# A row-sum kernel whose last load is split in two by partitions

## The chip, the cores and the metric

The kernel runs on one core of a Trainium2 chip. The metric is device time in microseconds of one execution; the kernel before has three such times. Beside them there is one profiled execution, from which all spans, waits and lengths below are taken.

## The reference

The kernel sums the last axis of a float32 array of 32 x 512 x 1024. Seen flat, these are 16,384 rows of 1024 numbers, 67.1 MB to be read, and 16,384 sums, 66 KB, to be written.

```python
def setup_inputs():
    batch, seq, dim = 32, 512, 1024
    return {"x": np.random.randn(batch, seq, dim).astype(np.float32)}

def reference(x):
    return np.sum(x, axis=-1).astype(np.float32)
```

## The kernel before, in words

Each of the 128 partitions owns 128 rows: 112 of the body (`x_a`, results in `res_a`) and 16 of the end (`x_z`, results in `res_z`). The rows of one partition lie one behind the other in memory.

The body goes through three buffers `xt0` to `xt2`, sixteen rows a partition each, seven blocks in all. Every block comes by two loads, of the even and of the odd partitions (64 each), that share one semaphore of the buffer; the very first row of each partition comes ahead of them by a load of its own (`first`). VectorE sums a block with one reduction (`rows_dve`, line 55). In the seventh block ScalarE takes seven of the sixteen rows, one at a time (`rows_act`, line 66).

The end's sixteen rows come in five loads. Three pieces of 9, 4 and 2 rows go into a body buffer (line 94); the last row of each partition goes into a tile of its own, `tail`, in two loads of all 128 partitions (lines 95 to 97): columns 0 to 543, and columns 544 to 1023, the latter 16 places further on so that there is room for a partial sum between them. VectorE and ScalarE share the first two pieces by rows; of the third each takes one row. For the last row VectorE adds the two halves of a stretch to one another and sums the result (`pairs_dve`, line 73, one addition and one read of the accumulator). This is done twice: first for columns 0 to 543, whose sum is written just ahead of the remaining 480 columns, behind a zero in the gap, and then for those 480 columns with that sum and the zero before them (482 numbers, 241 pairs). The second addition therefore waits for its load (line 126) and for VectorE's own earlier result (line 127).

All loads and both stores are issued by SP in the order of the list `loads` (lines 131 to 134): a load into a buffer that was in use waits for the reduction that frees it. The five end loads follow at once on one another, since they go into one freed buffer and into `tail`, which was free from the start. After them SP waits for the first tail load, for the body's sums on VectorE and on ScalarE, and issues the store of `res_a`; then for all sums, and issues the store of `res_z` (lines 135 to 141). At the very end it clears the semaphores. Three of the loads are moved ahead of the program's opening barrier.

Of the kernel before, what the change touches and what calls it, by code (L numbers as in the profile page):

```python
# [10 lines left out]
G = 16  # L11
BUFS = 3
ACT_ROWS = 7
CUT = 544
CUTS = (0, 9, 13, 15)
EARLY = 3


def row_sums(nc, x: bass.AP, out: bass.AP):
    P = nc.NUM_PARTITIONS  # L20
    x_flat = x.flatten_outer_dims()
    R, D = x_flat.shape
# [4 lines left out]
    def block(r0, n):  # L27
        x_b = x_flat[r0 : r0 + P * n].rearrange("(p c) d -> p (c d)", p=P)
        out_b = out_flat[r0 : r0 + P * n].rearrange("(p c) -> p c", p=P)
        return x_b, out_b  # L30

    x_a, out_a = block(0, BODY)
    x_z, out_z = block(P * BODY, G)

    def sbuf(name, n):
        return nc.alloc_sbuf_tensor(name, [P, n], F32)

    xt = [sbuf(f"xt{i}", G * D) for i in range(BUFS)]
    tail = sbuf("tail", D + 16)
# [2 lines left out]
    res_z = sbuf("res_z", G)  # L42

    names = [f"slot{i}" for i in range(BUFS)] + ["first", "piece0", "piece1", "piece2", "tail0"]
    names += ["tail1", "vec", "act", "early_store", "store"]
    sems = {n: nc.alloc_semaphore(n) for n in names}
    slots = [sems[f"slot{i}"] for i in range(BUFS)]
    vec, act = sems["vec"], sems["act"]
# [22 lines left out]
    def pairs_dve(t, a, b, acc, pairs):  # L71
        h = (a + b) // 2
        nc.vector.tensor_tensor_reduce(  # L73
            out=pairs[:, 0 : h - a], in0=t[:, a:h], in1=t[:, h:b], scale=1.0, scalar=0.0,
            op0=ADD, op1=ADD, accum_out=acc,
        ).then_inc(vec, 1)
        count["vec"] += 1
# [5 lines left out]
    loads = []  # L83
    for b in range(n_bufs):
# [4 lines left out]
        for q, i, s in parts:  # L89
            k = 1 if s is sems["first"] else G  # L90
            loads.append((b, xt[b % BUFS][q, i * D : k * D], x_a[q, (c + i) * D : (c + k) * D], s))
    last = xt[n_bufs % BUFS]
    for k, (i, j) in enumerate(zip(CUTS, CUTS[1:])):
        loads.append((n_bufs, last[:, i * D : j * D], x_z[:, i * D : j * D], sems[f"piece{k}"]))
    for k, (i, j, gap) in enumerate(((0, CUT, 0), (CUT, D, 16))):
        e = (G - 1) * D
        loads.append((0, tail[:, i + gap : j + gap], x_z[:, e + i : e + j], sems[f"tail{k}"]))


    nc.vector.memset(tail[:, CUT + 15 : CUT + 16], 0.0).then_inc(vec, 1)  # L100
    count["vec"] += 1
# [11 lines left out]
    for k in range(2):  # L113
        i, j = CUTS[k], CUTS[k + 1]
        h = (j - i) // 2
# [8 lines left out]
    nc.vector.wait_ge(sems["tail0"], 16)  # L124
    pairs_dve(tail, 0, CUT, tail[:, CUT + 14 : CUT + 15], pairs[0])
    nc.vector.wait_ge(sems["tail1"], 16)
    nc.vector.wait_ge(vec, count["vec"])
    pairs_dve(tail, CUT + 14, D + 16, res_z[:, 15:16], pairs[1])

# [19 lines left out]
def kernel(tc: tile.TileContext, x: bass.AP, out: bass.AP):  # L149
    tc.close()  # L150
    tc.compile()  # L151
    nc = tc.nc
    row_sums(nc, x, out)

    sp = mybir.EngineType.SP
    fn = nc.m.functions[0]
    entry, body = None, None
    for blk in fn.blocks:  # L160
        ops = [i for i in blk.instructions if i.engine == sp]
        if entry is None:
            entry = blk
        elif any(i.opcode == "DMACopy" for i in ops):
            body = blk
            break
    code = list(body.instructions)
    loads = [i for i in code if i.engine == sp and i.opcode == "DMACopy"][:EARLY]
    for load in loads:
        assert not load.sync_info.on_wait  # L170
        code.remove(load)
    body.instructions = code
    code = list(entry.instructions)
    at = next(k for k, i in enumerate(code) if i.engine == sp and i.opcode == "Drain")
    code[at:at] = loads
    entry.instructions = code
# [29 lines left out]
```

## Time and profile before

| | us |
|---|---|
| Three executions, median | 162.22 |
| lowest and highest | 161.07, 162.95 |
| Profiled execution, span from its first to its last instruction | 159.6 |
| VectorE busy in it | 121.4 (76%) |
| ScalarE busy in it | 17.2 (11%) |
| Bytes moved, and mean rate over the span | 67.18 MB, 421 GB/s |
| Share of the 16 DMA engines' span that the load and store queue took | 98.1% |
| Issue of the last load, and time to its landing | 118.37, 39.3 |

The span is counted from the first to the last of the program's own instructions; the executions' times also hold what lies around it, 2.6 us by the median. A load's time to landing runs from its issue on SP to the moment when all sixteen increments of its semaphore are there; for loads that are queued behind others most of it is waiting in the queue. Starts in what follows are microseconds from the start of the span.

### The profile page before, as it was taken

The page shows a single profiled execution, that of the slowest core. Times are in us where ns is not written, and L with a number is a line of the kernel's source. Part 1 is how long each engine was busy: PE and PEld are TensorE (multiplying, and loading weights), DVE is VectorE, ACT ScalarE, POOL GpSimd, SP SyncE. Part 2 cuts the span into 40 slices and gives each one's busy share as a digit, 9 for nine tenths or more (in the row PEclk, how much of TensorE's full clock was granted, in tenths as well). Part 3 has the DMA queues.
Part 4 walks back from the last instruction along what each step waited for, and adds up shares of the span by engine and source line. Part 5 has one row for each costly group of instructions (what it writes and reads, how often), then busy time and mean ns, then how long its engine had stood idle before and what let it go on. Part 6 is the DMA issues. An engine that isn't in the chain of part 4 may idle for free.

```text
span 159.6 us, 114 instructions
## 1 busy us (share of the span) xinstructions
DVE 121.4 (76%) x16; ACT 17.2 (11%) x31; POOL 0.2 (0%) x4
## 2 busy tenths in 40 slices
DVE  0000049998699968999599994999949999499685
ACT  2000000000000000000000000000000000494694
POOL 0000000000000000000000000000000000000000
DMA  9988996996996997998969969969969969699994
GB/s 378 493 370 370 493 526 263 526 509 279 526 509 279 526 460 329 526 411 378 526 263 526 526 263 526 526 263 526 509 279 526 509 279 526 296 443 443 390 401 145
DMA packets 2273, 67.18 MB, mean 421 GB/s; under 512 B 609, under 2 KB 737, under 8 KB 993
## 3 DMA queue, kind: packets, MB, share of 16 engines
q1 hardware_dynamic: 2272, 67.18, 98.1%
q14 instruction: 1, 0.00, 0.0%
HBM read 67.11 MB, written 0.07 MB: 421 GB/s over the span
## 4 chain that ended last, share of the span: by engine, by line
DMA 74%; DVE 22%; SPq 2%; issue 0%
DMA xt<-in_x_dram 49%; DMA tail<-in_x_dram 25%; DVE res_a L55 22%; SPq L134 2%; DVE pairs L73 0%; DVE res_z L73 0%
## 5 line engine op out<-in xcount | busy, mean ns | idle before, releaser
L55 DVE TENSOR_REDUCE res_a<-xt 128x16 f32<-128x16384 f32 (+1 forms) x7 | 113.1, 16154 | 31.6 <-DMA xt<-in_x_dram 31.6
L66 ACT ACTIVATE xt<-xt 128x1024 f32<-128x1024 f32 x15 | 15.6, 1044 | 137.5 <-DMA xt<-in_x_dram 137.5
L55 DVE TENSOR_REDUCE res_z<-xt 128x4 f32<-128x4096 f32 (+1 forms) x2 | 6.7, 3353 | 1.8 <-DMA xt<-in_x_dram 1.8
L66 ACT ACTIVATION_READ_ACCUMULATOR xt<-xt 128x1 f32 x15 | 2.8, 188 | 0.0
L100 DVE MEMSET tail<- 128x1 f32 x1 | 0.1, 59 | 3.0 <-PEq L151 3.0
L66 ACT ACT_TABLE_LOAD x1 | 1.3, 1283 | 2.9 <-PEq L151 2.9
L73 DVE CUSTOM_DVE_ANT_0 pairs<-tail 128x272 f32<-128x272 f32 (+1 forms) x2 | 0.9, 427 | 0.1
L73 DVE CUSTOM_DVE_ANT_0 pairs<-xt 128x512 f32<-128x512 f32 x1 | 0.7, 692 | 0.2 <-DMA xt<-in_x_dram 0.2
L73 DVE DVE_READ_ACCUMULATOR2_ANT res_z<- 128x1 f32 x2 | 0.2, 83 | 0.0
L190 POOL MEMSET const-bfloat16-1.0<- 128x1 bf16 x1 | 0.1, 102 | 0.0
L190 POOL MEMSET const-uint8-127<- 128x1 uint8 x1 | 0.1, 102 | 0.0
L190 POOL MEMSET const-float32-1.0<- 128x1 f32 x1 | 0.1, 99 | 0.0
L190 POOL MEMSET const-float32-0.0<- 128x1 f32 x1 | 0.1, 98 | 0.2 <-issue 0.2
L73 DVE DVE_READ_ACCUMULATOR2_ANT tail<- 128x1 f32 x1 | 0.1, 83 | 0.0
## 6 DMA issues: line engine op xcount, KB each, us to landing
xt<-in_x_dram SPq DMA_DIRECT2D x2, 3840.0 KB, 16.6
xt<-in_x_dram SPq DMA_DIRECT2D x1, 4608.0 KB, 32.5
xt<-in_x_dram SPq DMA_DIRECT2D x1, 2048.0 KB, 37.0
xt<-in_x_dram SPq DMA_DIRECT2D x1, 1024.0 KB, 39.0
xt<-in_x_dram SPq DMA_DIRECT2D x1, 512.0 KB, 3.7
tail<-in_x_dram SPq DMA_DIRECT2D x1, 272.0 KB, 39.2
tail<-in_x_dram SPq DMA_DIRECT2D x1, 240.0 KB, 39.3
xt<-in_x_dram SPq DMA_DIRECT2D x12, 39.0
```

The source lines that it names most:

```text
L55: nc.vector.tensor_reduce(out=res[:, c : c + n], in_=t[:, j * D : (j + n) * D].rearrange("p (j d) -> p j d", d=D), axis=X, op=ADD,).then_i ...
L66: nc.scalar.activation(out=v, in_=v, func=COPY, accum_out=res[:, c + i : c + i + 1]).then_inc(act, 1)
L73: nc.vector.tensor_tensor_reduce(out=pairs[:, 0 : h - a], in0=t[:, a:h], in1=t[:, h:b], scale=1.0, scalar=0.0, op0=ADD, op1=ADD, accum_out ...
L100: nc.vector.memset(tail[:, CUT + 15 : CUT + 16], 0.0).then_inc(vec, 1)
L134: nc.sync.dma_start(out=dst, in_=src).then_inc(s, 16)
L190: nc = _bacc.Bacc("TRN2", target_bir_lowering=False, num_devices=1)
```

## The change

The second load of the last row, columns 544 to 1023 of all 128 partitions, is replaced by two: first partitions 120 to 127, then partitions 0 to 119. The second of them has a new semaphore, `tail2`, and VectorE's last addition waits for it too. Nothing else is touched: the tiles, the bytes, the other loads and the store's conditions stay.

```diff
+WIDE = 120
...
-    names += ["tail1", "vec", "act", "early_store", "store"]
+    names += ["tail1", "tail2", "vec", "act", "early_store", "store"]
...
-    for k, (i, j, gap) in enumerate(((0, CUT, 0), (CUT, D, 16))):
-        e = (G - 1) * D
-        loads.append((0, tail[:, i + gap : j + gap], x_z[:, e + i : e + j], sems[f"tail{k}"]))
+    e = (G - 1) * D
+    ends = ((0, CUT, 0, slice(0, P)), (CUT, D, 16, slice(WIDE, P)), (CUT, D, 16, slice(0, WIDE)))
+    for k, (i, j, gap, q) in enumerate(ends):
+        loads.append((0, tail[q, i + gap : j + gap], x_z[q, e + i : e + j], sems[f"tail{k}"]))
...
     nc.vector.wait_ge(sems["tail1"], 16)
+    nc.vector.wait_ge(sems["tail2"], 16)
     nc.vector.wait_ge(vec, count["vec"])
     pairs_dve(tail, CUT + 14, D + 16, res_z[:, 15:16], pairs[1])
```

## Prediction

> **What bounds the kernel now.** I read the page first, for who is busy; then the chain of waits, for what ends last; then the timeline of the last 3 us, the only stage that the change can reach. The page's part 4 says:
>
> ```profile
> DMA 74%; DVE 22%; SPq 2%; issue 0%
> DMA xt<-in_x_dram 49%; DMA tail<-in_x_dram 25%; DVE res_a L55 22%; SPq L134 2%; DVE pairs L73 0%; DVE res_z L73 0%
> ```
>
> The reader is to see that transfers carry the chain, and that the 22% of VectorE are no rival: a reduction stands there because it frees the buffer that a queued load needs, not because data waits for it. Part 3 gives the load queue 98.1% of sixteen engines' span. So time is bytes over rate (67.18 MB at a mean of 421 GB/s is 159.6 us), plus what happens after the last byte. The change moves the same bytes; only the end can change.
>
> The end of the chain of waits:
>
> ```profile
> 118.37 39.30 DMA tail<-in_x_dram
> 157.68 0.03 issue
> 157.71 0.41 DVE pairs L73
> 158.12 0.01 DVE res_z L73
> ```
>
> Columns are start, length, what. The last load of the row's tail was issued at 118.37 and landed 39.30 later, at 157.68; VectorE took up its last addition 0.03 later. Taken alone this says: make that load land earlier and all behind it moves. The timeline of VectorE just before says how far:
>
> ```profile
> 156.43 0.69 DVE L73 CUSTOM_DVE_ANT_0 pairs<-xt 128x512 f32<-128x512 f32 x1 [0.20 <-DMA xt<-in_x_dram]
> 157.05 0.08 DVE L73 DVE_READ_ACCUMULATOR2_ANT res_z<- 128x1 f32 x1
> 157.12 0.44 DVE L73 CUSTOM_DVE_ANT_0 pairs<-tail 128x272 f32<-128x272 f32 x1
> 157.48 0.08 DVE L73 DVE_READ_ACCUMULATOR2_ANT tail<- 128x1 f32 x1
> 157.71 0.41 DVE L73 CUSTOM_DVE_ANT_0 pairs<-tail 128x241 f32<-128x241 f32 x1
> ```
>
> VectorE is busy without a break from 156.43 to 157.56 (157.48 plus 0.08). The last addition uses what the one before wrote, so it cannot start earlier whatever lands. The idle time before it is 157.71 - 157.56 = 0.15 us, and the wait for VectorE's own result (line 127, in the trace as a 21 ns instruction that ends at 157.62) fills the first 0.06 of it. In the one other place where VectorE passes such a wait and then starts (the first reduction) 0.05 lies between. So the earliest start is about 157.67: **the change can gain 0.04 us here at most**.
>
> Why would the split load land at another time at all? The answer on DMA for the stretch 156.9 to 157.4, in 40 slices of 12.5 ns:
>
> ```profile
> DMA  0408040307000004000003000003000000000000
> DMA packets 18, 0.02 MB, mean 38 GB/s; under 512 B 8, under 2 KB 18, under 8 KB 18
> ```
>
> A row of 480 columns is one packet of 1920 bytes, counted in the slice where it starts. Up to 157.02 several engines send; then a single one starts three more, six slices apart: 75 ns a row, 3 x 75 = 0.23 us behind the rest. The trace's semaphore record says the same. Each load is told in sixteen increments, one an engine: of this load fifteen lie between 157.12 and 157.44 and the last is at 157.68, 0.24 later. The first load has 3.46 and then 3.72, the last body load 137.72 and then 137.97. One engine is thus late by a constant amount from the first load on; its pace is that of the others. Which of the sixteen it is, or whether it is the same one in other executions, the trace does not say.
>
> **The change part by part.**
>
> *One more load on SP.* A tail issue takes 442 to 454 ns. The new one delays the 120-row load's issue from 118.37 to about 118.86. Behind them on SP stands the wait before the store of the body's results (28.9 us idle, then 9.3 more for the first tail load). The cover is 39 us of queued data; cost 0. Without that cover it would be 0.49.
>
> *The bytes at the end.* Where an engine served 8 rows of the last 480 columns (0.59 from the landing of the first tail load, 157.09, to 157.68), some engines now serve one row of the 8-row load and then their part of the 120-row load. The extra row costs 0.075 plus one more completion packet (9 ns in the trace): 0.084. How the chip spreads 8 and 120 rows the trace does not show: every load in it has 128 or 64 rows, and all of those are spread evenly (sixteen increments inside 0.6 us). The bounds by these rows are 8 rows an engine on fifteen engines, as now (0.6 us), and all 120 on one (120 x 0.075 = 9.0). I take the first, since it is what both row counts seen do; the second is kept as a rival.
>
> *Where the late engine falls* then decides. (i) It gets nothing of the last load: the rest is in by 157.44, with an extra row 157.52; VectorE's own 157.67 becomes the bound: -0.04. (ii) It gets 8 rows: landing 157.68 as now, 0 from the transfer. (iii) It gets 9: 157.76, +0.08.
>
> *One more wait on VectorE.* Line 129 adds a semaphore to the two that the last addition waits for. Behind it on VectorE stands only that addition, and for it the result's store. The built program still has one addition there; its semaphores rise from two to three. The separate wait for VectorE's own result is there already, and SP's wait at line 137 carries two semaphores in one instruction, so I take no new instruction: 0. The upper bound is the first reduction, which waits for two loads' semaphores: landing 21.85, start 21.95, so 0.10 where the single-wait case takes 0.03: +0.07. Below zero is excluded, since a longer list of conditions releases nothing earlier.
>
> *Stores.* The store of the body's results still hangs on the first tail load (157.11), ahead of both; its packets move from 157.95 on, after the last tail byte. The result's store follows the last addition: issued 158.16, landed 159.57. Both keep their distance to what they wait for.
>
> **Sum:** (i) -0.04, (ii) 0 to +0.07, (iii) +0.08 to +0.15. The profiled execution goes from 159.6 to between 159.56 and 159.75. The median of the runs, 162.22, lies 2.6 above that span (what lies around it, and their scatter: 161.07 to 162.95). I take case (ii) at no cost, between the two others: **162.2 us**.
>
> [...]
>
> **The rivals.**
>
> *Slower: 120 rows don't spread.* If the last load falls on k engines, it takes 120/k x 0.075 in place of 0.60. For k = 8 that is 1.13, +0.5 us; for 4, 2.25 and +1.65; for 1, 9.0 and +8.4, some 170.6. It passes 1% (1.62 us, about what a measurement of this kernel can tell from no change) at four engines or fewer. For it: no load in the trace has a row count that isn't a multiple of 16. Against it: 64 rows spread as evenly as 128. Over 1%: 0.06.
>
> *Faster: the late engine sets more than one landing.* If its 0.24 us could be had in full, the span were 159.36. Against it: the load of columns up to 544, the 2048-column piece and every load before keep all 128 rows, so VectorE's unbroken 156.43 to 157.56 still begins at the late engine's pace. Even a late engine ten times as late would delay those too. Worth 0.04, chance of its being seen as such nil.
>
> *The change doesn't do what it says:* the late engine keeps 8 or 9 rows and the split costs 0 to 0.15 (cases ii and iii): 162.2 to 162.4. It shares the side of the forecast.
>
> **How the numbers follow.** Cases (i) to (iii) together 0.92. Counting engines, a late one drawn at random is left out in 1 case of 16 and takes the extra row in 8 of 16; one that is late because it stands at the end of an order would be left out. I give (i) 0.26, (ii) 0.34, (iii) 0.32; they lie within 0.2 us of each other, so the forecast hardly depends on it. The rival of few engines 0.08, of which 0.06 over 1%. The runs of before scatter by -0.7% and +0.45% round their median, so a median of after may by chance fall past 1%: 0.04 on each side, taken from the cases. Chances: faster 0.04, same 0.86, slower 0.10. The range goes from the lowest run less 0.04, 161.0, to the highest plus 0.15 plus the 0.5 of eight engines, 163.6; it leaves out only the spreads on four engines or fewer.
>
> **What the profile after would show.** A row of 240 KB becomes one of 225 and one of 15. Case (i): fifteen increments in the last load, none late, VectorE's last addition at about 157.67 and a wait ended by itself. (ii) or (iii): one engine still alone at the end, the start at 157.71 to 157.86. Few engines: a long end with several lone packets 75 ns apart. I am wrong if the span moves by over 0.2 us, or if the loads before the tail change pace: nothing that I know of in the profile would do that.

## The result and the profile after

The changed kernel takes 162.32 us (median of 22 executions, 161.17 to 163.97) against 161.28 us (22 executions, 160.51 to 163.44): a ratio of 1.0054, 95% interval 1.0034 to 1.0073, or 0.9 us slower. The ratio is taken over the fast executions alone, those within 1.5% of the fastest of their kernel, which is why it comes to less than the 1.04 us between the medians. The loss is within 1% and the time lies inside the range that was given, but it is clear of no change, and no change is what was forecast. That 162.32 meets the forecast 162.2 is luck, as the section on the prediction tells. The profiled execution spans 160.7 us, 1.1 more than the one before.

Part 4 of the page after, the shares of the chain:

```profile
DMA 74%; DVE 22%; SPq 1%; issue 0%; DVEq 0%
DMA xt<-in_x_dram 49%; DMA tail<-in_x_dram 25%; DVE res_a L56 21%; SPq L137 1%; DVE pairs L74 1%; DVEq L130 0%; DVE tail L74 0%; DVE res_z L74 0%
```

The shares tell nothing new: transfers carry the chain as before. The end of the chain tells more (start, length, what):

```profile
118.03 40.05 DMA tail<-in_x_dram
158.08 0.02 issue
158.10 0.44 DVE pairs L74
158.54 0.02 DVE tail L74
158.56 0.03 issue
158.59 0.05 DVEq L130
158.64 0.09 issue
158.72 0.41 DVE pairs L74
```

The load on the chain is no longer the last one. It was issued at 118.03 and is the first tail load, columns 0 to 543, which the change left alone. It lands at 158.08, where it landed at 157.09 before. VectorE in the same stretch:

```profile
154.40 2.29 DVE L56 TENSOR_REDUCE res_z<-xt 128x2 f32<-128x2048 f32 x1 [0.44 <-DMA xt<-in_x_dram]
157.06 0.69 DVE L74 CUSTOM_DVE_ANT_0 pairs<-xt 128x512 f32<-128x512 f32 x1 [0.38 <-DMA xt<-in_x_dram]
158.10 0.44 DVE L74 CUSTOM_DVE_ANT_0 pairs<-tail 128x272 f32<-128x272 f32 x1 [0.34 <-DMA tail<-in_x_dram]
158.72 0.41 DVE L74 CUSTOM_DVE_ANT_0 pairs<-tail 128x241 f32<-128x241 f32 x1 [0.17 <-DVE tail L74]
```

From 156.43 to 157.56 VectorE worked without a break before; now it waits 0.38 us for the two-row piece and 0.34 us for the first tail load. Both loads stand ahead of the changed ones in the queue.

The engines' side, in stretches of half a microsecond (length, busy time and instructions of VectorE, ScalarE and GpSimd, clock, mean busy share of the DMA engines, GB/s). Before:

```profile
156.50:157.00 0.50, 0.50 (x1) 0.50 (x1) 0.00 (x0) 1.00 0.82 312
157.00:157.50 0.50, 0.50 (x4) 0.50 (x2) 0.00 (x0) 1.00 0.05 19
```

After:

```profile
156.50:157.00 0.50, 0.19 (x1) 0.42 (x2) 0.00 (x0) 1.00 0.98 358
157.00:157.50 0.50, 0.44 (x1) 0.44 (x1) 0.00 (x0) 1.00 0.63 159
```

Before, a full share moves 312 / 0.82 = 380 GB/s at these small packets; after, from 157.0 on, 159 / 0.63 = 252. The engines are busy and move less. The trace's packet record says the same row by row: all 128 packets of 1920 bytes took 79 ns before; after, 55 of them took over 90 ns ("long" in what follows), these 116 on average and 149 at most.

Two theories could hold after this. **Extra load**: one more load with its issue, completion and wait costs the time. **Destination**: 120 rows (and 8) are dealt to the engines in another way than 128, so that several engines write into the same group of partitions at one time; packets stretch, those of earlier loads on a late engine among them (a "late" engine is one whose increment comes last in every load). That engines meet in this way is a guess: packets bear no engine's name, so no record shows which engine writes where. Increments bear none either; each is read here as one engine's, since a load of 128 rows has sixteen of them and the profile counts sixteen engines. The 4-byte packets of the load and store queue agree: 352 before, sixteen for each of 22 loads and stores, and 359 after, seven more, where a load with sixteen increments gives way to two with eight and fifteen behind their rows.

One thing that neither theory names stands in the record. Counted from the landing of the four-row piece, the first tail load lands 0.54 us later than before (3.70 against 3.16), and most of that comes behind its packets. Its last packet of 2176 bytes ends at 156.72 before and its last increment is there at 157.09, 0.4 us later; after the change these are 157.28 and 158.08, 0.8 us. Three of its 128 packets are stretched, by 0.14 us in all. What a load waits for between its last packet and its last increment, the trace does not say.

### The profile page after: what moved, and what is told of

It reads as the page before. It is cut to its first block, busy times and chain, and to the rows that moved or that the text cites. A ratio compares the mean times of both kernels' runs of the same rounds, so it can differ in the third digit from the quotient of the medians.

```text
span 160.7 us, 115 instructions
## 1 busy us (share of the span) xinstructions
DVE 121.4 (76%) x16; ACT 17.2 (11%) x31; POOL 0.2 (0%) x4
## 4 chain that ended last, share of the span: by engine, by line
DMA 74%; DVE 22%; SPq 1%; issue 0%; DVEq 0%
DMA xt<-in_x_dram 49%; DMA tail<-in_x_dram 25%; DVE res_a L56 21%; SPq L137 1%; DVE pairs L74 1%; DVEq L130 0%; DVE tail L74 0%; DVE res_z L74 0%
```

## Experiments

Executions of one kernel scatter by up to 3 us here (last section), so beside each ratio a second measure is given that this scatter hardly touches: the **tail stretch**, from the start of the two-row reduction to the start of the last addition in the kernel's own profile. Both starts are rows of the timeline. Before it is 157.71 - 153.95 = 3.76 us (the first start from this row of the timeline before), after 158.72 - 154.40 = 4.32.

```profile
153.95 2.29 DVE L55 TENSOR_REDUCE res_z<-xt 128x2 f32<-128x2048 f32 x1 [0.44 <-DMA xt<-in_x_dram]
```

Each stretch is of one profile. Edits are shown against the changed kernel, that of the 120 rows alone against the kernel before.

| kernel | ratio (95% interval) | tail stretch, us | 1920-byte packets over 90 ns |
|---|---|---|---|
| before | | 3.76 | 0 of 128 |
| before again | 1.0012 (0.9977 to 1.0047) | 3.74 | 0 of 128 |
| changed | 1.0054 (1.0034 to 1.0073) | 4.32 | 55 of 128 |
| changed again | 1.0041 (1.0012 to 1.0069) | 4.43 | 41 of 128 |
| cut by columns, twice | 1.0011 (0.9979 to 1.0043), 0.9999 (0.9972 to 1.0027) | 3.83, 3.86 | none (960 bytes, all 44 ns) |
| odd and even partitions | 1.0009 (0.9981 to 1.0038) | 3.83 | 0 of 128 |
| contiguous halves | 1.0038 (1.0018 to 1.0058) | 4.37 | 77 of 128 |
| 112 and 16 rows | 1.0035 (1.0023 to 1.0047) | 4.14 | 68 of 128 |
| 120 rows, other source | 1.0049 (1.0033 to 1.0065) | 4.31 | 59 of 128 |
| 120 rows alone, twice | 1.0037 (1.0002 to 1.0072), 1.0039 (1.0011 to 1.0068) | 4.41, 4.44 | 39 and 30 of 120 |
| 8 rows added, twice | 1.0052 (1.0014 to 1.0091), 0.9999 (0.9979 to 1.0019) | 3.95, 3.97 | 4 and 3 of 136 |
| 8 rows added, far apart | 1.0036 (1.0005 to 1.0068) | 3.88 | 12 of 136 |
| cut moved to the two-row piece | 1.0240 (1.0223 to 1.0257) | 6.31 | 8 of 128 (and of 8192 bytes: 119 of 128 over 330 ns) |

### Before again

The kernel before, with no edit.

> The kernel before, unchanged, for a second profile of it. Both theories: ratio 1.000 within its interval, rows of 1920 bytes at 79 ns a packet, the first tail load 0.7 us behind the last piece on the latest engine. If its profile shows the body's last blocks late by 0.3 us as the changed kernel's did, that part is scatter and not the change.

Its tail repeats to 0.02 us: 3.74, no packet of 1920 bytes over 79 ns. Its two-row reduction starts at 153.97, before it was 153.95, after 154.40; so the body did not show the changed kernel's 0.45 us here. But the same point stands at 155.63 and 154.18 in two runs of the cut by columns, which leaves the body alone just as well, and at 153.69 in the run with another source, which has the changed kernel's cut. I count these 0.45 us as scatter between executions.

### A cut by columns

```diff
-    ends = ((0, CUT, 0, slice(0, P)), (CUT, D, 16, slice(WIDE, P)), (CUT, D, 16, slice(0, WIDE)))
+    MID = (CUT + D) // 2
+    ends = ((0, CUT, 0, slice(0, P)), (CUT, MID, 16, slice(0, P)), (MID, D, 16, slice(0, P)))
```

> The last 480 columns in two loads again, but cut by columns (240 and 240), each of all 128 partitions: one load, one issue and one wait more, as in the changed kernel, with the spread of the rows over the engines left alone. Extra-load theory (one more load, its completion and its wait cost the time): as slow as the changed kernel, ratio about 1.005. Spread theory (120 and 8 rows are dealt to the engines in another way than 128, and their packets hinder each other and the load before them): ratio 1.000 to 1.001, no packet of the tail stretched beyond its usual length.

> The cut by columns once more, for a narrower interval beside the changed kernel. Destination theory: 1.000 to 1.001 and below the changed kernel clear of both intervals. If the extra load, its issue and its wait carry a good part of the loss: 1.003 or more.

The two ratios are 1.0011 and 0.9999, no packet is stretched, and the tail stretch is 3.83 and 3.86. VectorE in the second run:

```profile
154.18 2.29 DVE L56 TENSOR_REDUCE res_z<-xt 128x2 f32<-128x2048 f32 x1 [0.46 <-DMA xt<-in_x_dram]
156.69 0.69 DVE L74 CUSTOM_DVE_ANT_0 pairs<-xt 128x512 f32<-128x512 f32 x1 [0.22 <-DMA xt<-in_x_dram]
157.35 0.44 DVE L74 CUSTOM_DVE_ANT_0 pairs<-tail 128x272 f32<-128x272 f32 x1
158.04 0.41 DVE L74 CUSTOM_DVE_ANT_0 pairs<-tail 128x241 f32<-128x241 f32 x1 [0.24 <-DMA tail<-in_x_dram]
```

One load and one wait more cost 0.07 to 0.12 us, and all of it stands ahead of the last addition (0.24 us idle); the two loads before it come as they did (VectorE waits 0.19 and 0.22 us for the first of them, 0.20 before, and in neither run for the second). Most of it is the wait: from the last increment to the start of the addition it is 0.12 and 0.11 us in the two runs (159.34 to 159.46, 157.93 to 158.04), 0.03 before the change (157.68 to 157.71). The intervals of the two ratios overlap the changed kernel's, so it is the packets and the stretch that make the difference, not the ratio alone. The extra-load theory falls.

### The two halves of the change, one at a time

The 120-row load alone, the last 480 columns of partitions 120 to 127 left out:

```diff
-    for k, (i, j, gap) in enumerate(((0, CUT, 0), (CUT, D, 16))):
+    for k, (i, j, gap, q) in enumerate(((0, CUT, 0, slice(0, P)), (CUT, D, 16, slice(0, 120)))):
...
-        loads.append((0, tail[:, i + gap : j + gap], x_z[:, e + i : e + j], sems[f"tail{k}"]))
+        loads.append((0, tail[q, i + gap : j + gap], x_z[q, e + i : e + j], sems[f"tail{k}"]))
...
+    nc.vector.memset(tail[96:P, CUT + 16 :], 0.0).then_inc(vec, 1)
+    count["vec"] += 1
```

> The 120-row load alone; the last 480 columns of partitions 120 to 127 are left out (zeros are added in their place). One load and one wait as before the change. Spread theory: the stretched packets (100 to 149 ns for 1920 bytes) stay, and so does most of the loss, ratio 1.003 to 1.005. Extra-load theory: the loss is gone, ratio 1.000 or a little under, since 15 KB less are moved.

> The 120-row load without the 8-row load once more (the last 480 columns of partitions 120 to 127 left out). If the 120-row load carries the loss: as the changed kernel within 0.15 us. If the 8-row load ahead of it carries a part, by its own meeting of eight rows and by the ninth row on eight engines: 0.1 to 0.3 us less than the changed kernel.

It moves fewer bytes, has no extra load and no extra wait, and is slower all the same: 1.0037 and 1.0039, a tail stretch of 4.41 and 4.44. In the first run its ends are:

```profile
154.50 2.29 DVE L55 TENSOR_REDUCE res_z<-xt 128x2 f32<-128x2048 f32 x1 [0.46 <-DMA xt<-in_x_dram]
158.91 0.41 DVE L73 CUSTOM_DVE_ANT_0 pairs<-tail 128x241 f32<-128x241 f32 x1
```

The semaphore record gives what eight rows an engine (120 rows, fifteen increments at the end) cost here: from the first increment of the first tail load to the first of the 120-row load's fifteen it is 157.24 - 156.25 = 0.99 us, and 0.98 in the second run; with the 128-row load before the change it is 157.12 - 156.53 = 0.59. The 120-row load is enough to bring the loss.

The 8 rows as an addition, into a spare tile, the last load whole:

```diff
+    spare = sbuf("spare", D + 16)
...
-    ends = ((0, CUT, 0, slice(0, P)), (CUT, D, 16, slice(WIDE, P)), (CUT, D, 16, slice(0, WIDE)))
+    ends = ((0, CUT, 0, slice(0, P)), (CUT, D, 16, slice(WIDE, P)), (CUT, D, 16, slice(0, P)))
...
+        to = spare if k == 1 else tail
+        loads.append((0, to[q, i + gap : j + gap], x_z[q, e + i : e + j], sems[f"tail{k}"]))
```

> The 8-row load is added, into a spare tile, and the last load keeps all 128 partitions: one load, one wait and 15 KB more than before. If the 8-row load is to blame (its eight rows meet at a few destinations, or its completion is slow): ratio 1.003 or more. Spread theory with the 120-row load to blame: ratio 1.000 to 1.001 (0.08 to 0.2 us for the extra row), the last load's packets at 79 ns.

> The 8-row load of partitions 120 to 127 once more as an addition, into a spare tile, the last load whole. By its profile (one more row behind the late engine's first tail load, 0.06 to 0.19 us, and the longer wait, 0.09): 1.001 to 1.002. If the 8-row load by itself carries half of the loss or more: 1.003 and above, its interval clear of 1.002.

The same with partitions 0, 16, 32 to 112 (`slice(0, P, 16)`):

> The same addition of 8 rows, but of partitions 0, 16, 32 to 112, so that they are written to places far apart. Destination theory: its eight packets at 79 ns and a ratio of 1.000 to 1.0015, not above the run with adjacent partitions. If a load on eight engines is slow in itself: the same ratio as with adjacent partitions.

The ratios don't agree with one another (1.0052, then 0.9999, then 1.0036 for the far-apart rows) and settle nothing: the first would blame the 8-row load, by what was expected of it, and the repeat lies below what was expected of it. The tail stretch does repeat: 3.95 and 3.97, some 0.2 us over before, of which 0.07 to 0.12 is the extra load and wait as such; the rows far apart give 3.88. So the 8-row load costs about 0.1 us of its own, near the 0.08 of the forecast. Whether that hangs on its partitions being adjacent, a difference of 0.07 to 0.09 between single profiles doesn't show. The destination theory's own expectation for the far-apart rows, all packets at 79 ns, failed: 12 are long, up to 109 ns.

### Which rows are cut off: 64, 112, 120

Odd and even partitions, 64 rows each; contiguous halves, 64 rows each; 112 and 16 rows:

```diff
-    ends = ((0, CUT, 0, slice(0, P)), (CUT, D, 16, slice(WIDE, P)), (CUT, D, 16, slice(0, WIDE)))
+    ends = ((0, CUT, 0, slice(0, P)), (CUT, D, 16, slice(1, P, 2)), (CUT, D, 16, slice(0, P, 2)))
```

```diff
-    ends = ((0, CUT, 0, slice(0, P)), (CUT, D, 16, slice(WIDE, P)), (CUT, D, 16, slice(0, WIDE)))
+    ends = ((0, CUT, 0, slice(0, P)), (CUT, D, 16, slice(64, P)), (CUT, D, 16, slice(0, 64)))
```

```diff
-WIDE = 120
+WIDE = 112
```

> The last 480 columns cut into odd and even partitions, 64 rows each, two apart, as the body's loads are, which move 65,536 bytes a packet in 2418 ns on every engine at once. Same rows per load and same engines as the contiguous halves, other destinations. Destination theory: 79 to 90 ns a packet, and a ratio of 1.000 to 1.0015. If any cut by partitions is slow: 120 ns and more as with the contiguous halves, and 1.003 to 1.005.

> The last 480 columns cut by partitions into two contiguous halves, 64 to 127 and then 0 to 63, four rows an engine in each if 64 rows are dealt to sixteen engines. Destination theory (packets stretch where more engines than usual write into the same group of partitions at one time): stretched packets in both halves, 100 to 160 ns for 1920 bytes, and a loss of 0.3 to 0.8 us behind the first tail load. Uneven-engines theory (only loads that use fewer than sixteen engines are slow): 79 ns, no loss over 0.1 us.

> The cut at partition 112 in place of 120: 16 rows and 112 rows, so that both can use all sixteen engines, one and seven rows each. Uneven-engines theory: packets at 79 ns, landing as before. Destination theory: 112 rows are dealt in another order than 128 too, so 1920-byte packets of 100 to 150 ns stay, and the late engine's 2176-byte packets stretch over their usual 88 ns.

Halves and odd/even are the pair that decides most. They have the same number of rows a load, sixteen increments in each, and the same bytes; only the partitions differ (and with them the rows read, which the next experiment takes up). Odd/even, VectorE and half a microsecond of the engines (columns as above):

```profile
153.87 2.29 DVE L56 TENSOR_REDUCE res_z<-xt 128x2 f32<-128x2048 f32 x1 [0.47 <-DMA xt<-in_x_dram]
157.70 0.41 DVE L74 CUSTOM_DVE_ANT_0 pairs<-tail 128x241 f32<-128x241 f32 x1 [0.21 <-DMA tail<-in_x_dram]
```

```profile
156.50:157.00 0.50, 0.50 (x2) 0.50 (x1) 0.00 (x0) 1.00 0.55 204
```

Contiguous halves:

```profile
153.73 2.29 DVE L56 TENSOR_REDUCE res_z<-xt 128x2 f32<-128x2048 f32 x1 [0.47 <-DMA xt<-in_x_dram]
157.37 0.44 DVE L74 CUSTOM_DVE_ANT_0 pairs<-tail 128x272 f32<-128x272 f32 x1 [0.45 <-DMA tail<-in_x_dram]
158.10 0.41 DVE L74 CUSTOM_DVE_ANT_0 pairs<-tail 128x241 f32<-128x241 f32 x1 [0.28 <-DMA tail<-in_x_dram]
```

```profile
156.50:157.00 0.50, 0.41 (x2) 0.50 (x1) 0.00 (x0) 1.00 0.81 158
```

A full share moves 204 / 0.55 = 371 GB/s with odd and even partitions, as before the change, and 158 / 0.81 = 195 with the halves. Rows spread over all partitions: 79 ns each. Rows of one half: 144 ns on average for the 77 long ones. The halves, like the changed kernel, make VectorE wait for the first tail load (0.45 us), which comes ahead of them. One 2176-byte packet of that load is over 100 ns (124); its last packet ends at 156.44, but its last increment comes at 157.34, 0.9 us later, where odd and even partitions have 156.57 and 157.02, 0.45. With 112 and 16 rows, both of which give sixteen increments, 68 packets are long: uneven use of the engines is not the cause either. The stretched 2176-byte packets expected there did not come (one, of 119 ns); the first tail load's last increment came late all the same, 0.75 us behind its last packet.

### Another source

```diff
+        src = x_flat[0:WIDE, i:j] if k == 2 else x_z[q, e + i : e + j]
-        loads.append((0, tail[q, i + gap : j + gap], x_z[q, e + i : e + j], sems[f"tail{k}"]))
+        loads.append((0, tail[q, i + gap : j + gap], src, sems[f"tail{k}"]))
```

> The changed kernel with another source for the 120-row load: columns 544 to 1023 of the first 120 rows of x, 4 KB apart, in place of the last row of each partition, 64 KB apart; the sums of the last row are therefore others. Destination the same. Source theory (the order of the reads makes packets slow): packets of the 120-row load back at 79 ns. Destination theory: they stay at 100 to 150 ns.

Rows 4 KB apart in place of 64 KB change nothing: 59 long packets, up to 159 ns, stretch 4.31. So the distance between the rows read is not what slows them; what is left of these theories is which partitions are written, and by which engine at what time; the second part no record shows. The same rows read into other partitions were not run.

### The cut moved to a larger load

```diff
-        loads.append((n_bufs, last[:, i * D : j * D], x_z[:, i * D : j * D], sems[f"piece{k}"]))
+        for q, m in ((slice(WIDE, P), "tail2"), (slice(0, WIDE), "piece2")) if k == 2 else ((slice(0, P), f"piece{k}"),):
+            loads.append((n_bufs, last[q, i * D : j * D], x_z[q, i * D : j * D], sems[m]))
...
+    ends = ((0, CUT, 0, slice(0, P)), (CUT, D, 16, slice(0, P)))
...
+    nc.scalar.wait_ge(sems["tail2"], 16)
     nc.scalar.wait_ge(sems["piece2"], 16)
...
+    nc.vector.wait_ge(sems["tail2"], 16)
     nc.vector.wait_ge(sems["piece2"], 16)
...
-    nc.vector.wait_ge(sems["tail2"], 16)
```

> The cut at partition 120 moved from the last 480 columns to the two-row piece before (8 KB a partition, 8192 bytes a packet at 309 ns), the last load whole again. Packets of the 120-row load some 1.4 to 1.6 times as long by the destination theory, that is 430 to 490 ns, and the piece lands 1.0 to 1.5 us later, partly kept to the end: ratio 1.005 to 1.010. Theory of a fixed cost for a cut load: no stretch, the same 0.5 to 0.9 us as in the changed kernel. If neither: 309 ns and ratio 1.000 to 1.002.

More than was expected: ratio 1.024, 3.7 us by medians (164.47 against 160.78). The engines while the 120-row piece runs (columns as above):

```profile
154.60:155.60 1.00, 0.94 (x1) 0.94 (x1) 0.00 (x0) 1.00 0.95 211
155.60:156.60 1.00, 1.00 (x1) 1.00 (x3) 0.00 (x0) 1.00 0.95 219
156.60:157.60 1.00, 0.34 (x1) 0.24 (x2) 0.00 (x0) 1.00 0.99 221
```

211 to 221 GB/s with the engines 95 to 99% busy is half of the 421 of the whole kernel before. Packets that took 309 ns take 647 on average, where they are long. The loss grows with the size of the cut load (0.9 us with 225 KB in the 120-row load, 3.7 with 960 KB), as a rate has it and a fixed cost does not. VectorE's waits in this run (the last row is the end of the tail stretch):

```profile
154.66 2.29 DVE L56 TENSOR_REDUCE res_z<-xt 128x2 f32<-128x2048 f32 x1 [1.43 <-DMA xt<-in_x_dram]
159.77 0.69 DVE L74 CUSTOM_DVE_ANT_0 pairs<-xt 128x512 f32<-128x512 f32 x1 [2.83 <-DMA xt<-in_x_dram]
160.97 0.41 DVE L74 CUSTOM_DVE_ANT_0 pairs<-tail 128x241 f32<-128x241 f32 x1
```

The first of these waits is for the four-row piece, which stands ahead of the cut one. All its packets had ended by 153.31, its last increment came at 154.63, 1.3 us later; before the change it was 0.35 (153.58, 153.93). A load can thus be held up with all its packets done, and the tail stretch of 6.31, which starts behind this wait, leaves that part out.

The contiguous halves ran at about half of what odd and even partitions reached (195 against 371 GB/s per full share), and the 120 rows, in the larger load here, at half of the whole kernel's rate. That engines crowd at their destination is no more than a guess at the cause: it needs engines that write neighbouring rows in step, which no record here shows. The same guess, with four neighbouring rows an engine, would have the odd and the even partitions crowd as well, and in them no packet is long. So the runs show which cuts are slow, and not why.

### The changed kernel again

No edit.

> The changed kernel, unchanged, beside the next three on one chip, for a second profile. Destination theory: stretched 1920-byte packets again, ratio 1.004 to 1.006 as on record; if no single engine is far behind this time, the first tail load lands as before the change and the whole loss stands behind it, 0.2 to 0.4 us by the 120-row load, the rest in the late engine's earlier packets.

This profile shows a second way in which the loss reaches the end, since its late engines are further behind. VectorE:

```profile
155.50 2.29 DVE L56 TENSOR_REDUCE res_z<-xt 128x2 f32<-128x2048 f32 x1 [0.46 <-DMA xt<-in_x_dram]
158.66 0.69 DVE L74 CUSTOM_DVE_ANT_0 pairs<-xt 128x512 f32<-128x512 f32 x1 [0.87 <-DMA xt<-in_x_dram]
159.93 0.41 DVE L74 CUSTOM_DVE_ANT_0 pairs<-tail 128x241 f32<-128x241 f32 x1 [0.17 <-DMA tail<-in_x_dram]
```

The two-row piece, two loads ahead of the changed ones, lands 158.64 - 155.48 = 3.16 us after the piece before it; without the change it was 156.41 - 153.93 = 2.48. The packet record shows why: two late engines (two increments lag in this run, last section) still send this piece's 8192-byte packets while the others are in the 120-row load, and four of these packets take 429 to 562 ns in place of 309 (three in a row: 520, 496, 429). The last rows themselves then come at 79 ns, when no other engine is left in the load. Here most of the loss is taken by packets of engines that have not yet reached the changed load; in the first profile it lay mostly between the first tail load's last packet and its last increment.

## Why the prediction was right or wrong

- **The number** was met by luck. The forecast took the median of three executions, 162.22, as the time before and added nothing; 22 executions put the time before at 161.28, and the change added 0.9. The two errors cancel to 0.1 us. Nor do 2.6 us lie around the span: where one execution has both, it is 1.3 to 1.4 (162.03 and 160.7 after, 160.95 and 159.6 in the repeated kernel before).
- **What bounds the kernel** held: the end only, 0.9 us of 161.
- **"The change can gain 0.04 us here at most"** held as a bound, and no cut gained anything.
- **The extra issue on SP** cost nothing: the three tail issues stand at 118.03, 118.50 and 118.93, and the cut by columns is not slower by a measurable amount (1.0011 and 0.9999).
- **The spread of the rows** was right by count. The semaphore record of the 8-row load has one increment half a microsecond after its issue (119.01) and eight from 157.09 to 157.73; that of the 120-row load one at 119.43 and fifteen from 157.83 to 158.48. Read as one engine an increment, that is eight and fifteen engines.
- **The step that failed is the price of a row.** "8 rows an engine on fifteen engines, as now (0.6 us)" took the 75 ns a row of a 128-row load for a row of any load. The long rows take 116 to 137 ns on average, and the term of 0.6 us measures 0.98 and 0.99 with the 120 rows alone. The other bound, 9.0 us, was reached by crowding all rows on one engine; that packets of the same size could take longer was on neither side.
- **The second failure follows from it.** The rival of a late engine was put aside because the loads ahead "keep all 128 rows", and the text closed with the loads before the tail changing pace as something that nothing in the profile would do. They did, and nearly all the time is lost there: from the landing of the four-row piece to that of the first tail load it is 3.16 us before (153.93 to 157.09), 3.70 and 3.80 in the two profiles after (154.38 to 158.08, 155.48 to 159.28). Part of it is an engine's stretched packets (in the first profile three of 88 ns, 0.14 us longer in all), part the longer time from the last packet to the last increment (0.8 us there, 0.4 before). In place of 0 to 0.15 us the tail stretch grew by 0.56 and 0.67 us in two profiles, and the result's store took 0.07 more (issued 159.17, landed 160.65; before 158.16 and 159.57). That sum, 0.63 to 0.74 us, lies within the measured 0.55 to 1.18 (0.34 to 0.73% of 161.28).
- **The extra wait** lies just over its upper bound: it was taken at 0 with +0.07 above and measures 0.08 to 0.09 with the cut by columns (0.11 and 0.12 from landing to start, 0.03 before).
- **The ninth row** (0.084) was about right, as far as single profiles tell: 0.1.
- **Where the late engine falls**: no one case. In the changed kernel's first profile the 8-row load is complete at 157.73 and the first tail load only at 158.08, so its late engine is none of those eight. In the first profile with 8 rows added, seven of eight are in by 157.21 and the last at 159.58, behind the first tail load's 159.39: there the late engine is one of the eight. A fixed cut cannot relieve an engine that changes. That an engine at the end of an order is left out, as the chances had it, was the author's estimate: no run shows an order of the engines.
- **The rival of few engines** took the right sign for another reason: not four engines at full pace but fifteen at some six tenths of it (0.59 against 0.99 us).

## What to carry to other kernels

Before a load is cut by partitions, ask where its rows are written, not only how many engines share them: with 64 rows, odd and even partitions ran at full pace (371 GB/s per full share, 79 ns a packet) and contiguous halves at about half (195 GB/s, 144 ns for the long packets). A cut by columns leaves the pattern alone and cost 0.1 us here. And a load that was slow in this way also delayed loads ahead of it in the queue here, by stretched packets of an engine that was still working on them (429 to 562 ns in place of 309), and by increments that came 0.75 to 1.3 us after their last packet in place of 0.35 to 0.45.

## What the runs showed beyond this

In some of these executions one DMA engine falls behind in the first microseconds and stays behind by that amount to the end. In the first run of the cut by columns the first body load has fifteen increments by 12.92 and the last at 14.59; at the last load the gap is 159.34 - 157.67, still 1.67 us. One engine began its body packets there at 4.19 where the others began by 3.01. The gap was 0.14 us in the repeated kernel before, 0.24 in its first profile and 2.18 with 8 rows added, with spans of 159.6, 159.6 and 162.1. In the second profile of the changed kernel, span 161.9, two engines lag: the last stands 1.36 behind the third-last (14.37 and 13.01). This may explain much of why executions of one kernel lie up to 3 us apart, but only one execution of a run has a trace; what holds the engine up was not tried.
